# One decoder trunk on one core: product pairs added in one PSUM bank, tokens scaled before they are turned, kept projection weights, later folds, and a tail by 256 tokens

## The chip, the cores and the metric

The kernel runs on one core of a Trainium2 chip. The metric is the device time of one execution in microseconds (us): 2147.15 us before, the median of three runs (2144.82 to 2148.33). The engines are called as the profile calls them: PE (TensorE's matmuls), PEld (its weight loads), DVE (VectorE), ACT (ScalarE), POOL (GpSimd) and SP (SyncE, which issues most transfers).

## The reference, cut to what matters

The stream is 1024 tokens by 1024 channels in float32, and there are two layers. The first has a short gated convolution and a gated feed-forward network (FFN), the second multi-head latent attention and another FFN.

```python
h = h + short_conv_mixer(rms_norm(h, conv_norm_g), w_in, conv_w, w_out)   # u = h @ w_in, split in gate_b, gate_c, val
h = h + swiglu_ffn(rms_norm(h, conv_ffn_norm_g), w13, w2)                 # (silu(g) * u) @ w2
k_nope, k_pe, v = shared_mla_kv(h, ...)
h = h + mla_mixer(rms_norm(h, mla_norm_g), ...)                           # 8 heads, causal, then attn @ w_o
h = h + swiglu_ffn(rms_norm(h, mla_ffn_norm_g), w13, w2)
return rms_norm(h, final_norm_g)
```

`rms_norm` divides each token by the root of its mean square and multiplies by a gain per channel.

## The kernel before, in words

Channels lie on the 128 partitions and tokens run along the free dimension. Every float32 operand is cut in a high part, cast by ACT (L111, L306, L367), and a low part, the difference, made by DVE (L112, L307, L371). A product is then three matmuls in place of one (`three`, L152 to L155: high by high, high by low, low by high), each of 128x512.

The big weight products use a seven-product scheme on 2x2 blocks of weights and tokens. `Quad` is one pair of column blocks. Its seven products have the numbers 1, 2, 5, 6, 7, 4, 3, and each is 12 matmuls into a PSUM bank of its own (`product`, L422). After each, `evict` (L431) adds the bank to the result tiles C1 and C2: product 1 is copied by ACT (L437), 2 is added to it by DVE (L434), 5 is copied negated by ACT (L444) and subtracted by DVE (L445), 6 is subtracted by DVE (L447), and so on. `up` (L470) lays out the products of all quads, twelve for the convolution's input product and 22 for each FFN. The first seven quads (`head`) have their products 1 and 2 first, while the second half of the tokens is still being normed; the others run one after another. `Down` (L630) is the same scheme for the FFN's second product, with four banks per product and its operands loaded again from DRAM. `Plain` (L520) is the ordinary product for the output projections.

Between the stages stands a `Boundary` (L720). For each half of 512 tokens it squares the stream (ACT, L711), folds the squares of the channel blocks (DVE, L715), sums them over the partitions by matmuls with ones (`token_sums`, L214), makes one over the root (`rsqrt`, L194 to L206), spreads it by another matmul (`bcast`, L230), and multiplies it into the stream (DVE, L291).

The order is written out by hand. `Steps` holds a list of PE steps, and each other instruction is put before or after one of them; every engine then gets its instructions in that order and takes them strictly one after another. Only the attention is ordered by a scheduler. PSUM has eight banks of 128x512, handed out in turn. Raw weights have five buffers.

The places that are spoken of:

- **Beginning** (`first_x`, L830). Eight tiles of 128 tokens arrive. Four are turned by PE into channel order and written to DRAM as the residual (`raw_x`). The norm of the first 512 tokens is then multiplied in by a matmul with a diagonal matrix (L849). The second 512 are scaled as they lie (`scaled`, L866) before the second step, and turned (L880).
- **Attention's end**. The last three of the eight heads' outputs stay in SBUF. Their projection weights are loaded and cut by `Plain`, once for each half of the tokens and of the columns.
- **Tail** (from L1511). The second FFN's last product adds to the last 512 tokens by 512 channels. The final norm needs all of them, then come turns to token order (`out_turn`, L1518), the scaling (`out_store`, L1520) and the stores of 128x512 by SP (L1527).

Of the kernel before, what the change touches and what calls it, by code (L numbers as in the profile page):

```python
# [48 lines left out]
def trunk(ctx, tc, aps, out):  # L49
# [102 lines left out]
    def three(ps, wh, wl, xh, xl, st, en):  # L152
        nc.tensor.matmul(ps, lhsT=wh, rhs=xh, start=st, stop=False)  # L153
        nc.tensor.matmul(ps, lhsT=wh, rhs=xl, start=False, stop=False)  # L154
        nc.tensor.matmul(ps, lhsT=wl, rhs=xh, start=False, stop=en)  # L155
# [8 lines left out]
    vrows = half_tile("vrows")[:, :P]  # L164
    nc.vector.memset(vrows, 0.0)
    nc.scalar.dma_start(ident, A["ident"])
    col, r0 = {}, 0
    for nm in ("conv_norm_g", "conv_w", "conv_ffn_norm_g", "kv_norm_g", "mla_norm_g", "kv_latent_norm_g",
               "mla_q_norm_g", "mla_ffn_norm_g", "final_norm_g"):
        a = A[nm]  # L170
        if len(a.shape) == 3:
            a = a.rearrange("a b c -> (a b c)")
        elif len(a.shape) == 2:
            a = a.rearrange("a b -> (a b)")
        n = a.shape[0] // P
        nc.gpsimd.dma_start(vrows[r0:r0 + n, :], a.rearrange("(r p) -> r p", p=P))
        col[nm] = r0
        r0 += n
# [15 lines left out]
    def rsqrt(sums, nt, dim):  # L194

        var = small.tile([P, KD], F32, name="var")[:, :nt]
        nc.vector.tensor_scalar(var, sums, 1.0 / dim, EPS, ALU.mult, ALU.add)
        r = small.tile([P, KD], F32, name="r")[:, :nt]
# [147 lines left out]
    class Quad:  # L346


        def __init__(self, wv, ca, cb, first, done, eng):

            self.wv, self.ca, self.cb, self.first, self.done, self.eng = wv, ca, cb, first, done, eng
            self.W, self.bank, self.early, self.made = {}, {}, False, None

# [33 lines left out]
        def half(self, i):  # L387

            if i in (5, 7, 3):
                self.box = hi_tile("w_hi"), lo_tile("w_lo")  # L390
            (hi, lo), o = self.box, 512 if i in (6, 4) else 0
# [30 lines left out]
        def product(self, i, X):  # L422
            h, l, o = self.W[i]
            self.bank[i] = ps1("q")
            for c in range(4):
# [3 lines left out]
                three(self.bank[i], h[:, ws], l[:, ws], xh[:, cs], xl[:, cs], c == 0, c == 3)  # L429

        def evict(self, name):  # L431

            b = self.bank.pop(name)
            add = lambda o, a: nc.vector.tensor_tensor(o, b, a, ALU.add)  # L434
            if name == 1:
                self.C1 = work("c1")
                nc.scalar.copy(out=self.C1[:, 512:], in_=b)  # L437
            elif name == 2:
# [19 lines left out]
        def add(self, steps, op, name):  # L458
# [4 lines left out]
            if name == 3:  # L463
                for j, fn in enumerate(self.done):
                    steps.after(n + 1 + j, lambda fn=fn: fn(self.C1, self.C2))
# [4 lines left out]
    def up(steps, quads, op):  # L470
# [5 lines left out]
        for x, i in [(a, 1), (b, 1), (a, 2), (b, 2), *((x, i) for x in head[2:] for i in (1, 2)),  # L476
                     *((x, i) for i in (5, 6, 7, 4, 3) for x in (a, b)),
                     *((x, i) for x in quads[2:] for i in ((5, 6, 7, 4, 3) if x in head else (1, 2, 5, 6, 7, 4, 3)))]:
            n[x, i] = x.add(steps, op, i)
        for x in head:  # L480
            if not x.early:
                steps.before(n[x, 1] - 9, x.load_a)
                steps.before(n[x, 1] - 3, x.pair_hi)
                steps.before(n[x, 1] - 2, x.pair_lo)
        for x in quads:
# [8 lines left out]
            else:  # L494
                steps.before(n5 - 11, x.load_a)
                steps.before(n5 - 10, x.load_b)
                steps.before(n5 - 6, x.pair_hi)
                steps.before(n5 - 5, x.pair_lo)
# [21 lines left out]
    class Plain:  # L520


        def __init__(self, steps, wv, groups, x, final):
            self.ends = []
# [4 lines left out]
        def product(self, steps, wv, groups, x, final, t, cb):  # L529
            banks, tail = [], []  # L530
            for g, ks in enumerate(groups):
# [11 lines left out]
                def one(c, q, box=box, g=g, ks=ks):  # L543
                    if not banks:
                        banks.extend(ps1("pl") for _ in range(4))
                    wh, wl = box["w"]
                    xh, xl = x.get(t, g, c)
                    ws = slice(c * 512 + q * P, c * 512 + (q + 1) * P)
# [4 lines left out]
                steps.before(s - 7, load)  # L553
                steps.before(s - (1 if tail else 2), parts)
                if cb == 0:
                    x.prepare(steps, s, t, g)
                if cb and g >= len(groups) - 2:
# [46 lines left out]
    class Kept:  # L604


        def __init__(self, O, groups):
            self.O, self.groups = O, groups
# [4 lines left out]
        def get(self, t, g, c):  # L613
            return [x[:, t * 512:(t + 1) * 512] for x in self.O[self.groups[g][c] - self.groups[0][0]]]
# [15 lines left out]
    class Down:  # L630


        def __init__(self, steps, m, ws, nk, w, final, keep=True):
# [7 lines left out]
        def product(self, steps, i):  # L641
            wb, mb, outs = SEVEN[i]
            banks, tail = [], []
            for g, ks in enumerate(self.groups):
# [24 lines left out]
                def one(c, q, box=box, ks=ks):  # L669
# [4 lines left out]
                    cs, ws = slice(c * 512, (c + 1) * 512), slice(c * 512 + q * P, c * 512 + (q + 1) * P)  # L674
                    three(banks[q], wh[:, ws], wl[:, ws], mh[:, cs], ml[:, cs], k == 0, k == self.half - 1)
# [8 lines left out]
                if i == 6 and g >= len(self.groups) - 2:  # L684
                    tail += [lambda q, c=c, one=one: one(c, q) for c in range(len(ks))]
                    continue
                for c in range(len(ks)):
                    s = steps.add(lambda c=c, one=one: [one(c, q) for q in range(4)])
            for q in range(4 if tail else 0):
# [13 lines left out]
    class Norm:  # L703


        def __init__(self):
            self.sq = [[], []]

        def add(self, n, t):
            sq = work("nsq")[:, :512]  # L710
# [3 lines left out]
            if len(a) > 2:  # L714
                nc.vector.tensor_tensor(a[0], a[0], a.pop(1), ALU.add)  # L715
# [4 lines left out]
    class Boundary:  # L720


        def __init__(self, gname):
            self.op, self.norm = Operand(gname), Norm()
# [14 lines left out]
        def second(self, steps, n):  # L739

            steps.before(n + 1, lambda: setattr(self, "d", diag(half_tile, self.norm.sums(1), 4)))
            steps.before(n + 3, lambda: setattr(self, "R1", bcast(self.d, 1)[0]))
            todo = self.op.second(lambda f, kk: self.op.block(f, 1, kk, self.R1))
            for m, fn in zip((3, 4, 5, 6, 6, 7, 8, 9, 11, 12, 13, 14, 15, 16, 17, 18), todo):
# [63 lines left out]
    def gains():  # L808
        vps = ps1("vps")
        nc.tensor.transpose(vps[:, :r0], vrows[:r0, :], ident[:r0, :r0])  # L810
# [763 lines left out]
```

## Time and profile before

| | before |
|---|---|
| median of three runs | 2147.15 us |
| the profiled execution, its time | 2144.56 us |
| its span, first to last instruction | 2142.6 us |
| mean granted TensorE clock | 0.990 |
| granted clock, 0 to 50 us | 0.90 |
| granted clock, 1450 to 1500 us | 0.84 |
| granted clock, 2100 us to the end | 0.89 |

The views have one row per instruction or group: its start or count, its duration, its engine, its line of the kernel, the tile written and the tiles read. In square brackets, or behind a bar, stands the time for which the engine had been idle and what ended that. Matmuls overlap, so that the duration of one (some 0.39 us for 128x512) is longer than the distance between two. The place of the distance is taken from the starts.

### The profile page before, as it was taken

Reading aid. Unit: us, or ns where it says so; the run is one execution under the profiler, and the core shown is the slowest. Engines: PE = TensorE matmul, PEld = TensorE weight load, DVE = VectorE, ACT = ScalarE, POOL = GpSimd, SP = SyncE. Lnnn points to the kernel's source line nnn. Section 1 sums busy time; section 2 is a strip of 40 time slices with the busy share of each in tenths; the row PEclk is TensorE's granted clock in tenths of the full one; section 3 lists DMA queues with packets and bytes.
Section 4 is the critical chain, followed back from the end, with each engine's and each line's share of the span. In section 5 each row is a group of like instructions: output and inputs, shape, how many; then the busy total and the mean of one; then the engine's idle time right before and its main releaser. Section 6 shows DMA issues by size and latency. Waiting matters only on the chain. (4 is left out here: it accounts for less than half of the span.)

```text
span 2142.6 us, 25826 instructions
## 1 busy us (share of the span) xinstructions
PE 2079.4 (97%) x9553; PEld 1712.4 (80%) x9553; DVE 1526.0 (71%) x2275; ACT 845.0 (39%) x1418; POOL 305.0 (14%) x413
## 2 busy tenths in 40 slices
PE   7999999999999999999999999989999999999997
PEld 6878888878888887787888887867878888888786
DVE  5897656977777778867577787357887777767545
ACT  6423344523333333354245455224433333333444
POOL 2233210121112210000013332100111111100000
PEclk9999999999999999999999999998999999999999
DMA  6354775476866686564122224225478475685542
GB/s 210 84 118 118 214 282 175 108 194 192 193 161 152 147 277 230 192 235 144 58 68 68 65 72 154 98 93 162 148 177 189 146 162 168 149 323 191 176 167 98
DMA packets 275565, 340.55 MB, mean 159 GB/s; under 512 B 18143, under 2 KB 178080, under 8 KB 275120
## 3 DMA queue, kind: packets, MB, share of 16 engines
q1 hardware_dynamic: 241376, 264.28, 37.9%
q0 software_dynamic: 33920, 74.57, 16.4%
q8 instruction: 74, 1.21, 0.2%
q14 instruction: 51, 0.42, 0.1%
q10 hardware_dynamic: 144, 0.07, 0.0%
HBM read 261.79 MB, written 126.35 MB: 181 GB/s over the span
## 5 line engine op out<-in xcount | busy, mean ns | idle before, releaser
L155 PE MATMUL q<-xh,w_lo 128*128 128x512 f32 x1568 | 614.6, 392 | 5.0 <-DVE w_lo L112 2.8
L153 PE MATMUL q<-xh,w_hi 128*128 128x512 f32 x1568 | 615.3, 392 | 1.5 <-ACT w_hi L111 1.5
L154 PE MATMUL q<-xl,w_hi 128*128 128x512 f32 x1568 | 612.5, 391 | 2.1 <-DVE xl L307 2.1
L155 PEld LDWEIGHTS q<-xh,w_lo 128*128 128x128 f32 x1568 | 295.4, 188 | 75.2 <-DVE w_lo L112 11.8
L153 PEld LDWEIGHTS q<-xh,w_hi 128*128 128x128 f32 x1568 | 295.6, 188 | 65.4 <-ACT w_hi L111 4.8
L154 PEld LDWEIGHTS q<-xl,w_hi 128*128 128x128 f32 x1568 | 295.7, 189 | 64.3 <-DVE xl L307 2.9
L112 DVE TENSOR_TENSOR w_lo<-wr,w_hi 128x512 fp32r<-128x512 f32 (+1 forms) x272 | 194.5, 715 | 162.4 <-ACT w_hi L111 162.3
L111 ACT CAST w_hi<-wr 128x512 fp32r<-128x512 f32 (+1 forms) x272 | 169.7, 627 | 286.9 <-DVE wr L385 136.7
L155 PE MATMUL dn<-mp_hi,wp_lo 128*128 128x512 f32 x616 | 242.6, 394 | 4.9 <-DVE wp_lo L112 3.2
L153 PE MATMUL dn<-mp_hi,wp_hi 128*128 128x512 f32 x616 | 242.3, 393 | 0.5 <-ACT wp_hi L111 0.5
L154 PE MATMUL dn<-mp_lo,wp_hi 128*128 128x512 f32 x616 | 240.8, 391 | 0.7 <-DVE mp_lo L112 0.7
L973 POOL COPY paced<-pace 128x1 f32<-128x1 f32 x128 | 73.7, 576 | 959.4 <-ACT pace L972 959.4
L112 DVE TENSOR_TENSOR mp_lo<-m,mp_hi 128x1024 fp32r<-128x1024 f32 x84 | 95.3, 1134 | 129.5 <-ACT mp_hi L111 129.5
L111 ACT CAST mp_hi<-m 128x1024 fp32r<-128x1024 f32 x84 | 82.2, 979 | 214.9 <-PE dn L154 206.4
L155 PEld LDWEIGHTS dn<-mp_hi,wp_lo 128*128 128x128 f32 x616 | 115.9, 188 | 36.3 <-DVE wp_lo L112 12.3
L154 PEld LDWEIGHTS dn<-mp_lo,wp_hi 128*128 128x128 f32 x616 | 116.0, 188 | 25.6 <-DVE mp_lo L112 1.1
L153 PEld LDWEIGHTS dn<-mp_hi,wp_hi 128*128 128x128 f32 x616 | 116.1, 188 | 24.8 <-ACT wp_hi L111 1.8
L456 ACT ACTIVATE c<-c 128x512 f32<-128x512 f32 x44 | 27.8, 632 | 234.9 <-DVE c L434 234.9
L434 DVE TENSOR_TENSOR c<-q,c 128x512 f32<-128x512 f32 x112 | 77.0, 687 | 49.4 <-PE q L155 44.8
L112 DVE TENSOR_TENSOR wp_lo<-w,wp_hi 128x1024 fp32r<-128x1024 f32 x84 | 94.8, 1128 | 0.0
L111 ACT CAST wp_hi<-w 128x1024 fp32r<-128x1024 f32 x84 | 81.9, 975 | 0.0
L1368 ACT ACTIVATE p<-ps_s,mx,rq 128x128 f32<-128x128 f32 (+3 forms) x64 | 53.3, 834 | 59.3 <-DVE mx L1365 54.1
(289 smaller groups left out, 3337.6 us busy)
## 6 DMA issues: line engine op xcount, KB each, us to landing
m<-md_f SPq DMA_DIRECT2D x70, 512.0 KB, 4.9
md_f<-c SPq DMA_DIRECT2D x110, 256.0 KB, 3.6
wr<-in_conv_ffn_w_dram SPq DMA_DIRECT2D x47, 512.0 KB, 6.5
wr<-in_mla_ffn_w_dram SPq DMA_DIRECT2D x47, 512.0 KB, 5.3
w<-mw_f SPq DMA_DIRECT2D x40, 512.0 KB, 3.7
h<-hd SPq DMA_DIRECT2D x32, 512.0 KB, 8.4
wr<-in_conv_w_in_dram SPq DMA_DIRECT2D x31, 512.0 KB, 5.6
mw_f<-in_conv_ffn_w_dram POOLq DMA_DIRECT2D x30, 512.0 KB, 7.1
```

Of the source, the lines that this page charges most:

```text
L111: nc.scalar.copy(out=hi, in_=src)
L112: (eng or nc.vector).tensor_tensor(lo, src, hi.bitcast(F32), ALU.subtract)
L153: nc.tensor.matmul(ps, lhsT=wh, rhs=xh, start=st, stop=False)
L154: nc.tensor.matmul(ps, lhsT=wh, rhs=xl, start=False, stop=False)
L155: nc.tensor.matmul(ps, lhsT=wl, rhs=xh, start=False, stop=en)
L434: add = lambda o, a: nc.vector.tensor_tensor(o, b, a, ALU.add)
L456: nc.scalar.activation(self.C1[:, 512:], self.C1[:, 512:], self.first)
L973: nc.gpsimd.tensor_copy(b, a)
L1368: nc.scalar.activation(p[:, :kw], ps[:, :kw], AF.Exp, bias=mx, scale=rq[:, qb:qb + 1], accum_out=rsum)
```

## The change

1. `up` gives every quad `onto = {2: 1, 6: 5}`: product 2 goes on in product 1's bank and 6 in 5's. The bank of 1 is copied by ACT before 2 begins, and then holds 1 + 2, which ACT takes out alone; 5 is no longer subtracted, and 6's eviction takes 5 + 6. Two DVE operations per quad go. So that ACT has a product's time for its copy, the order becomes 1, 5, 2, 6, 7, 4, 3, and 5, 4, 6, 7, 3 for the rest of the head quads.
2. The first 512 tokens are scaled as they lie too, in two halves of the channels, and turned by the identity. The fourth tile's residual is put off, the convolution's gain comes in a transfer of its own, and the squares, the norm and the scaling of the second 512 tokens go two to four steps later. The first two quads' convolution steps are spread (`apart = 2`).
3. The projection weights of heads 5 to 7 are loaded whole during the last head, cut once, and kept in six tiles.
4. At that boundary the squares of the second half of the tokens are not folded as they come, but by four folds some steps later (`later=True`), and the weights of the first two FFN quads are loaded and cut eight steps earlier (`up(..., 8)`).
5. The last three channel blocks of the last `Down` product run by 256 tokens (`finish_half`), each half with its own norm and stores; the first half's stores before it are closer together.

```diff
-        dg = half_tile("dg")
-        diagonals(dg, xs[0], 4)
         conv_quads[0].pair_hi()
+        scaled(0, slice(0, 512))
         conv_quads[0].pair_lo()
-        squares(4, 5)
...
+        first_block(0, 0)
+        first_block(0, 1)
+        xop.advance()
+        raw_store(3, last, (nc.vector, nc.scalar))
+        conv_quads[1].pair_hi()
+        scaled(0, slice(512, S))
+        conv_quads[1].pair_lo()
...
-    steps.before(1, scaled)
...
+    steps.before(1, lambda: first_block(1, 0), lambda: first_block(1, 1), xop.advance)
+    steps.before(2, lambda: squares(4, 5), lambda: gains(1))
+    steps.before(3, lambda: squares(6, 7), lambda: norms(1))
+    steps.before(4, lambda: scaled(1, slice(0, S)))
...
         def product(self, i, X):
             h, l, o = self.W[i]
-            self.bank[i] = ps1("q")
+            j = self.onto.get(i)
+            self.bank[i] = ps1("q") if j is None else self.bank[j]
...
         def evict(self, name):
+            elif name == 2 and name in self.onto:
+                nc.scalar.activation(self.C1[:, :512], b, self.first)
...
-                nc.vector.tensor_tensor(self.C1[:, 512:], self.C1[:, 512:], b, ALU.subtract)
+                if 6 not in self.onto:
+                    nc.vector.tensor_tensor(self.C1[:, 512:], self.C1[:, 512:], b, ALU.subtract)
...
+        for x in quads:
+            x.onto = {2: 1, 6: 5}
+        lead = [(x, i) for j in range(0, FILL, 2) for i in (1, 2) for x in head[j:j + 2]]
...
-                     *((x, i) for x in quads[2:] for i in ((5, 6, 7, 4, 3) if x in head else (1, 2, 5, 6, 7, 4, 3)))]:
+                     *((x, i) for x in quads[2:] for i in ((5, 4, 6, 7, 3) if x in head else (1, 5, 2, 6, 7, 4, 3)))]:
...
+    for k in (5, 6, 7):
+        wo_load(k)
+    wo_parts(5)
     for u in pend:
         pv(*u)
...
-    bd = Boundary("mla_ffn_norm_g")
-    pl = Plain(steps, kp(flat(A["mla_w_o"])), pairs(5, H), Kept(O1, pairs(5, H)), bd.norm.add)
+    bd = Boundary("mla_ffn_norm_g", later=True)
+    for j, k in enumerate((6, 7)):
+        steps.before(j, lambda k=k: wo_parts(k))
+    pl = Plain(steps, None, [[5], [6], [7]], Kept(O1), bd.norm.add, wo_kept)
...
-    n0 = up(steps, quads2, bd.op)
+    n0 = up(steps, quads2, bd.op, 8)
...
+                for th in range(2):
+                    for q in range(4):
+                        s = steps.add(lambda q=q, th=th: [fn(q, halves[th]) for fn in tail])
+                        steps.after(s, lambda q=q, th=th: self.by_half(q, th, lambda: add(q, th)))
...
+    steps.after(n + 7, last_mean, lambda: out_turn(5, 1), lambda: out_store(5, 1), lambda: out_store(4, 1), last_rows,
+                *[lambda a=a: out_turn(*a) for a in ((6, 0), (7, 0), (6, 1), (7, 1))],
+                *[lambda a=a: out_store(*a) for a in ((6, 0), (7, 0), (6, 1), (7, 1))])
```

The order on ACT at the beginning, before: from the last cast of the first 512 tokens to the scaling of the second 512 (`sq` are squares of token tiles `xt`, `c1` a product's copy, `w_hi` a cut weight whose raw tile is `wr`).

```order
L306 CAST xh_267<-xraw_254 128x1024
L852 ACTIVATE xraw_270<-xps_271,vec_69 128x512
L852 ACTIVATE xraw_270<-xps_277,vec_69 128x512
L306 CAST xh_284<-xraw_270 128x1024
L803 ACTIVATE sq_288,xsum_98<-xt_124 128x1024
L803 ACTIVATE sq_290,xsum_98<-xt_126 128x1024
L199 ACTIVATE r_294<-var_292 128x4
L437 COPY c1_322<-q_309 128x512
L367 CAST w_hi_324<-wr_303 128x1024
L870 ACTIVATE xt_122<-xt_122,rs_301 128x1024
L870 ACTIVATE xt_126<-xt_126,rs_301 128x1024
```

And now, from the first product's copy on:

```order
L451 COPY c1_277<-q_264 128x512
L378 CAST w_hi_279<-wr_256 128x1024
L929 ACTIVATE xraw_281<-xps_288,vec_69 128x512
L316 CAST xh_294<-xraw_281 128x1024
L929 ACTIVATE xraw_297<-xps_304,vec_69 128x512
L316 CAST xh_311<-xraw_297 128x1024
L451 COPY c1_328<-q_315 128x512
L378 CAST w_hi_332<-wr_258 128x1024
L872 ACTIVATE sq_334,xsum_98<-xt_120 128x1024
L872 ACTIVATE sq_336,xsum_98<-xt_122 128x1024
L453 ACTIVATE c1_277<-q_264 128x512
L872 ACTIVATE sq_358,xsum_98<-xt_124 128x1024
```

The squares of the second 512 tokens now stand behind two casts of weights, and the third quad's cast `w_hi_279` ahead of the operands of product 2. The bank `q_264` is read twice, after product 1 and after product 2.

The order on DVE at the boundary behind the attention, before: from the adding of the second half's first channel blocks (`h` from the banks `pl`) to the second quad operand (`xl` is the low part of an FFN operand, `nsq` a fold of squares).

```order
L715 TENSOR_TENSOR nsq_12221<-nsq_12221,nsq_12241 128x512
L291 SCALAR_TENSOR_TENSOR xraw_12252<-h_11455,vec_69,R0_12202 128x512
L291 SCALAR_TENSOR_TENSOR xraw_12252<-h_11495,vec_69,R0_12202 128x512
L569 TENSOR_TENSOR h_11455<-h_11455,pl_12146 128x512
L715 TENSOR_TENSOR nsq_12221<-nsq_12221,nsq_12245 128x512
L569 TENSOR_TENSOR h_11741<-h_11741,pl_12228 128x512
L715 TENSOR_TENSOR nsq_12221<-nsq_12221,nsq_12269 128x512
L307 TENSOR_TENSOR xl_12250<-xraw_12224,xh_12249 128x1024
L291 SCALAR_TENSOR_TENSOR xraw_12282<-h_11701,vec_69,R0_12202 128x512
L291 SCALAR_TENSOR_TENSOR xraw_12282<-h_11741,vec_69,R0_12202 128x512
L371 TENSOR_TENSOR w_lo_12285<-wr_12106,w_hi_12255 128x1024
L569 TENSOR_TENSOR h_11495<-h_11495,pl_12147 128x512
```

And now, at the same place:

```order
L595 TENSOR_TENSOR h_11586<-h_11586,pl_12092 128x512
L301 SCALAR_TENSOR_TENSOR xraw_12115<-h_11340,vec_69,R0_12065 128x512
L301 SCALAR_TENSOR_TENSOR xraw_12115<-h_11380,vec_69,R0_12065 128x512
L595 TENSOR_TENSOR h_11340<-h_11340,pl_12017 128x512
L595 TENSOR_TENSOR h_11626<-h_11626,pl_12093 128x512
L595 TENSOR_TENSOR h_11380<-h_11380,pl_12018 128x512
L595 TENSOR_TENSOR h_11706<-h_11706,pl_12094 128x512
L317 TENSOR_TENSOR xl_12113<-xraw_12087,xh_12112 128x1024
L301 SCALAR_TENSOR_TENSOR xraw_12154<-h_11586,vec_69,R0_12065 128x512
L301 SCALAR_TENSOR_TENSOR xraw_12154<-h_11626,vec_69,R0_12065 128x512
L595 TENSOR_TENSOR h_11746<-h_11746,pl_12095 128x512
L317 TENSOR_TENSOR xl_12152<-xraw_12115,xh_12151 128x1024
```

The folds and the cut of the weights have left this stretch; what remains between the operands are the adds of `h` and the multiplications.

The order on PE at the program's end, before (`dn` are the last product's banks, `fps` turns to token order, `sp` sums for the norm):

```order
L154 MATMUL dn<-mp_lo,wp_hi 128x512
L155 MATMUL dn<-mp_hi,wp_lo 128x512
L1518 MATMUL fps<-ident,h 128x128 x9
L214 MATMUL sp<-ones,nsq 128x1 x8
L1518 MATMUL fps<-ident,h 128x128 x7
```

And now:

```order
L154 MATMUL dn<-mp_lo,wp_hi 128x256
L155 MATMUL dn<-mp_hi,wp_lo 128x256
L224 MATMUL sp<-ones,nsq 128x1 x2
L1644 MATMUL fps<-ident,h 128x128 x4
L224 MATMUL sp<-ones,nsq 128x1 x2
L1644 MATMUL fps<-ident,h 128x128 x16
```

Behind the last product stand four sums in two pieces, where eight stood, and all turns of the last 256 tokens.

More of the change, by code (lines that the diff above doesn't have):

```diff
@@ L464, in add, with up @@
                 for j, fn in enumerate(self.done):
-                    steps.after(n + 1 + j, lambda fn=fn: fn(self.C1, self.C2))
+                    steps.after(n + 1 + j * self.apart, lambda fn=fn: fn(self.C1, self.C2))
             return n
     FILL = 7
-    def up(steps, quads, op):
+    def up(steps, quads, op, ahead=0):
         head, n0 = quads[:FILL], len(steps.pe)
@@ L520, in trunk, with __init__ @@
     class Plain:
[L523 to L524 removed]
+        def __init__(self, steps, wv, groups, x, final, kept=None):
+            self.ends, self.kept = [], kept
             for t in range(2):
@@ L552, in product @@
                 s = len(steps.pe)
-                steps.before(s - 7, load)
-                steps.before(s - (1 if tail else 2), parts)
+                if kept is None:
+                    steps.before(s - 7, load)
+                    steps.before(s - (1 if tail else 2), parts)
                 if cb == 0:
                     x.prepare(steps, s, t, g)
-                if cb and g >= len(groups) - 2:
+                if cb and (g >= len(groups) - 2 or kept is not None):
                     tail += [lambda q, c=c, one=one: one(c, q) for c in range(len(ks))]
@@ L684, in product @@
                 if i == 6 and g >= len(self.groups) - 2:
-                    tail += [lambda q, c=c, one=one: one(c, q) for c in range(len(ks))]
+                    tail += [lambda q, *ts, c=c, one=one: one(c, q, *ts) for c in range(len(ks))]
                     continue
@@ L703, in trunk, with __init__, fold, flush @@
     class Norm:
-        def __init__(self):
-            self.sq = [[], []]
-        def add(self, n, t):
+        def __init__(self, later=False):
+            self.sq, self.two, self.later = [[], []], {}, later
+        def fold(self, t):
+            a = self.sq[t]
+            nc.vector.tensor_tensor(a[0], a[0], a.pop(1), ALU.add)
+        def flush(self, t):
+            while len(self.sq[t]) > 1:
+                self.fold(t)
+        def add(self, n, t):
+            if t and self.later:
+                if n % 2 == 0:
+                    self.two[n // 2] = work("nsq")
+                    self.sq[1].append(self.two[n // 2])
+                nc.scalar.activation(self.two[n // 2][:, n % 2 * 512:n % 2 * 512 + 512], st.h[n][:, 512:], AF.Square)
+                return
             sq = work("nsq")[:, :512]
@@ L739, in second @@
         def second(self, steps, n):
-            steps.before(n + 1, lambda: setattr(self, "d", diag(half_tile, self.norm.sums(1), 4)))
-            steps.before(n + 3, lambda: setattr(self, "R1", bcast(self.d, 1)[0]))
+            m = 1
+            if self.norm.later:
+                for j in range(3):
+                    steps.before(n + 1 + j, lambda: self.norm.fold(1))
+                steps.before(n + 4, self.norm.last)
+                m = 5
+            steps.before(n + m, lambda: setattr(self, "d", diag(half_tile, self.norm.sums(1), 4)))
+            steps.before(n + m + 2, lambda: setattr(self, "R1", bcast(self.d, 1)[0]))
             todo = self.op.second(lambda f, kk: self.op.block(f, 1, kk, self.R1))
-            for m, fn in zip((3, 4, 5, 6, 6, 7, 8, 9, 11, 12, 13, 14, 15, 16, 17, 18), todo):
+            at = (8, 9, 9, 10, 11, 11, 12, *range(13, 22)) if self.norm.later else (3, 4, 5, 6, 6, 7, 8, 9, *range(11, 19))
+            for m, fn in zip(at, todo):
                 steps.before(n + m, fn)
```

238 lines of the change are left out of this document (148 added, 90 removed).

## The prediction

> **What bounds the kernel now.** I read the page first, then the busy time by stretches, then who PE waited for, and then the order of time at four places.
>
> ```profile
> span 2142.6 us, 25826 instructions
> PE 2079.4 (97%) x9553; PEld 1712.4 (80%) x9553; DVE 1526.0 (71%) x2275; ACT 845.0 (39%) x1418; POOL 305.0 (14%) x413
> ```
>
> PE is busy for nearly the whole span, so what can be won is what PE loses, and where.
>
> ```profile
> 0.00:50.00 50.00, 35.51 (x195) 31.11 (x196) 27.61 (x43) 33.23 (x49) 9.13 (x18) 0.90 0.71 224
> 100.00:150.00 50.00, 46.88 (x195) 35.42 (x193) 45.17 (x52) 14.29 (x27) 22.45 (x19) 1.00 0.54 120
> 450.00:500.00 50.00, 49.43 (x213) 39.08 (x212) 39.93 (x62) 16.48 (x35) 11.09 (x16) 1.00 0.81 196
> 1550.00:1600.00 50.00, 49.42 (x213) 39.21 (x212) 41.07 (x64) 13.72 (x28) 7.70 (x10) 1.00 0.80 199
> ...
> 1464.00:1490.00 26.00, 20.77 (x71) 15.77 (x70) 17.54 (x28) 10.20 (x15) 0.87 (x2) 0.74 0.60 189
> 1490.00:1550.00 60.00, 60.00 (x267) 49.66 (x266) 53.71 (x63) 29.38 (x46) 10.12 (x14) 1.00 0.42 129
> 2086.00:2104.00 18.00, 13.84 (x60) 11.14 (x59) 10.50 (x14) 10.36 (x14) 0.00 (x0) 0.91 0.53 185
> ```
>
> The columns after the stretch are PE, PEld, DVE, ACT and POOL with their counts, then the granted clock. From 1490 to 1550 nothing is lost: 267 matmuls of 128x512 in 60 us, one in 0.225 us, 222 in 50 us. By that rate 100 to 150 lost 27 matmuls or 6.1 us with DVE busy for 90%, 450 to 500 and 1550 to 1600 lost 2.0 us each. Most of the span runs at the full rate and can't be made faster by taking work off DVE or ACT.
>
> ```profile
> PE xps L880 <- DVE xt L872: 5.4, 1, 5.4
> PE fps L1518 <- DVE o L1526: 4.2, 1, 4.2
> ...
> PE ps_wo L146 <- DVE h L1444: 2.1, 1, 2.1
> ...
> PE q L155 <- DVE w_lo L371: 2.0, 1, 2.0
> ```
>
> The waits (total, times, longest) are few and sit at the beginning, at the boundary behind the attention and in the tail, and there the clock falls too.
>
> **The bank shared by two products.** It takes two DVE operations off each of 56 quads.
>
> ```profile
> L434 DVE TENSOR_TENSOR c<-q,c 128x512 f32<-128x512 f32 x112 | 77.0, 687 | 49.4 <-PE q L155 44.8 <-ACT xraw L881 3.1 <-issue 0.5
> L437 ACT COPY c<-q 128x512 f32<-128x512 f32 x56 | 32.8, 586 | 59.3 <-PE q L155 59.3
> ```
>
> Half of the first row goes, and as many subtractions of like shape: 112 x 0.69 = 77 us of DVE, nearly all of it hidden behind PE. It pays where DVE is late. In 100 to 150 some 2.65 quads run (50 us over 84 matmuls x 0.225), so DVE sheds 3.6 us of 45, and the first two quads' convolution steps no longer fall together: of 6.1 us lost I take 4 back (1 to 6). In the two FFN heads (450, 1550) I take back 3 of 4, between 2 lost and 4 won, as the new order 5, 4, 6, 7, 3 asks for its weights in another rhythm. The cover is one product: product 2 waits for ACT's copy of 1, which takes 0.59 us, while PE has 12 x 0.225 = 2.7 us of another product. The second row says that ACT stood waiting for PE ahead of these copies.
>
> **The beginning.**
>
> ```profile
> 10.40 0.19 ACT L803 ACTIVATION_READ_ACCUMULATOR sq<-xt 128x1 f32 x1
> 24.75 1.26 ACT L852 ACTIVATE xraw<-xps,vec 128x512 f32<-128x512 f32 x2
> 28.05 1.04 ACT L803 ACTIVATE sq<-xt 128x1024 f32<-128x1024 f32 x1
> 29.42 0.20 ACT L199 ACTIVATE r<-var 128x4 f32<-128x4 f32 x1 [0.24 <-DVE var L197]
> 30.00 1.05 ACT L367 CAST w_hi<-wr 128x1024 fp32r<-128x1024 f32 x1
> 30.94 2.19 ACT L870 ACTIVATE xt<-xt,rs 128x1024 f32<-128x1024 f32 x2
> ...
> 47.86 1.03 PE L880 MATMUL xps<-ident,xt 128*128 128x128 f32 x8
> ```
>
> ```profile
> L356 SPq DMA_DIRECT2D wr<-in_conv_w_in_dram x2: 486/4074/7663, 10.4 to 10.9; - x2
> ...
> DMA to landing us min/median/max: 15.9/16.5/17.1
> ```
>
> Before, the last turn ends at 48.9, with five products done. Now ACT carries the chain to the second half's norm. Behind the squares (10.6) it has two casts of weights and two of operands (0.95 apart, by 30.00 to 30.94), four scalings of 512 and two evictions (0.6 each, by the two in 1.26) and two copies (0.59): 8.6 us, and with some 3 us of waits for DVE's norm, PE's turns and the first product this ends at 22. Then stands the third quad's cast. Its transfer was issued at 10.4 and landed 15.9 later, at 26.3. The fourth tile's residual, written to DRAM ahead of it before, now comes later; I take 25. From there come two evictions, four casts, two copies and the four squares (1.05 each): 1.2 + 3.8 + 1.2 + 4.2 = 10.4, with some 1 us of waits 36.4. The norm takes 1.5 (29.42 to 30.94), two scalings 2.2: 40.1. The next turns, 1.03, end at 41.1, with the same five products done. Three groups of turns remain, 3.1 us, which before lay behind. So 48.9 - 44.2 = 4.7, and with a slow clock after waits I take 4 (1 to 8; 8 if the weights land by 22). The 32 diagonal matmuls, which the trace counts as 64, become 32 turns; that is inside this sum.
>
> **The attention's end and the boundary.** Two cuts of weights of 128x1024 now stand in DVE's queue around the last maximum, one of them ahead of the add of `h` on whose bank PE waited 2.1 us.
>
> ```profile
> L307 DVE TENSOR_TENSOR xl<-xraw,xh 128x1024 fp32r<-128x1024 f32 x42 | 52.1, 1243 | 2.8 <-ACT xh L306 2.8
> L715 DVE TENSOR_TENSOR nsq<-nsq 128x512 f32<-128x512 f32 x36 | 24.6, 684 | 0.1
> L569 DVE TENSOR_TENSOR h<-h,pl 128x512 f32<-128x512 f32 x32 | 21.7, 682 | 25.9 <-PE pl L155 25.9
> L291 DVE SCALAR_TENSOR_TENSOR xraw<-h,vec,R 128x512 f32<-128x512 f32 x16 | 11.2, 743 | 0.0
> ...
> 1396.70 0.73 PE L1361 MATMUL ps_s<-kh,qnh 128*128 128x512 f32 x2 [2.61 <-ACT p L1368]
> 1399.21 1.05 PE L1361 MATMUL ps_s<-KL,qrs 128*128 128x512 f32 x2
> ```
>
> By the first row, of a like shape, PE waits 1.2 us more there; the cuts that no longer stand ahead of the projection give some of it back, and a slow clock takes it: 1.5 lost in all (0 to 4). For a wait of 2.61 us was followed by matmuls 0.42 us apart (two in 1.05), some 1 us more in a handful. [...]
>
> From 1464 to 1490 stood 53 products, two spreads and 16 sums, which cost 55 x 0.225 + 2.0 (the sums in the tail, below) = 14.4; lost are 11.6, and about 1 in the first half's sums. Now the last DVE work before the first operand is an add and a low part, 0.6 + 1.2 after the twelfth step of the projection, while PE has nine matmuls or 2.0: no wait. The second operand comes behind two multiplications, one add and one low part, 1.3 + 0.6 + 1.2 = 3.1 us into a product that needs it after seven matmuls, 1.6: 1.5 lost. The other two follow after 1.3 + 1.2 + a fold of 1.2 + 1.2 at 8.0 us, where PE asks at 4.2 + 2.7 + 1.6 = 8.5. With two more folds, their last half and two weights (5.5 us) DVE is through at 13.5, and PE's sums stand at 4.2 + 4 x 2.7 = 15; half the sums go, 0.9. So 12.6 - 1.5 - 1 (clock) + 0.9 = 11 won, 9.5 with the attention's end (6 to 13).
>
> **The tail.**
>
> ```profile
> 1099.69 0.28 PE L1322 MATMUL ps_v<-wv_lo,lat_part 128*128 128x256 f32 x1
> 1099.81 0.28 PE L1323 MATMUL ps_v<-wv_hi,lat_part 128*128 128x256 f32 x1
> ...
> 2097.90 1.12 PE L1518 MATMUL fps<-ident,h 128*128 128x128 f32 x4 [4.16 <-DVE o L1526]
> ...
> 2129.31 0.69 DVE L696 TENSOR_TENSOR h<-h,dn 128x512 f32<-128x512 f32 x1 [0.75 <-PE dn L155]
> 2130.03 0.63 ACT L711 ACTIVATE nsq<-h 128x512 f32<-128x512 f32 x1 [0.66 <-DVE h L696]
> 2130.65 1.95 PE L214 MATMUL sp<-ones,nsq 128*128 128x1 f32 x16 [0.24 <-DVE nsq L715]
> 2132.64 0.16 DVE L197 TENSOR_SCALAR var<-sp 128x4 f32<-128x4 f32 x1 [2.04 <-PE sp L214]
> 2134.08 2.73 DVE L1526 TENSOR_SCALAR o<-fps,rs 128x512 f32<-128x512 f32 x4
> 2134.79 4.46 SPq L1527 DMA_DIRECT2D out_dram<-o  x8
> ```
>
> The wait of 4.16 us came as the last early store stood in DVE's queue behind the next product's operands, and its bank was wanted. The stretch from 2086 to 2104 has 48 products and 12 turns (0.11 each, as eight take 1.03 with the end of the last): 12.1 of 18 us, so 5.9 lost. The stores now end two steps before that product, and all of it goes; if not, 4 come back. From the last matmul (2129.3) to the norm's root chain were 3.3 us, then 1.4, then eight evictions on two engines and eight stores of 0.56 in line, with the end at 2142.6, 13.3 later. Now an add and a square of 256, 0.4 each by half of the rows above and their fixed share, and a quarter of the sums, 0.5: chain at 1.8, rows at 3.2, first store at 4.0, the fourth 1.7 later at 5.7. Before, 3.4 us passed from the last store's issue (2139.2) to the end; that makes 9.1. So 4.2 are won. Of 36 matmuls come 72 of 0.12 in place of 0.113: 0.5 lost; sums and turns inside the product 0.5 more; the first half's eight sums fewer win 0.9. In all 10 (6 to 12).
>
> **The sum.** 4 + 4 + 3 + 9.5 + 10 = 30.5 us off the profiled execution's 2144.56, which gives 2114.1. That execution lies 2.6 below the median of the runs, 2147.15; against the median the forecast is 2116.6. A difference of 0.2%, 4.3 us, is about what a measurement here can tell from none.
>
> **The rivals.**
> - *The banks tie PE to ACT* (slower, 5%). Every quad now has two places at which PE may not go on before ACT has copied, 112 in all. If ACT is late by 0.5 us at each, behind a cast that waits for DVE, that costs 56 us and gives 2172. It decides from 30.5 / 112 = 0.27 us on. For it: ACT takes its work strictly in order, and DVE makes it wait for long. Against it: the copy stands ahead of the next cast, and had 59.3 us of its own waiting for PE.
> - *The wait at the beginning only moves* (17%). The squares stand behind weights that may land at 26.3 or later, and ACT's chain with them; nothing is won there: 2120.6.
> - *DVE was not the limit* (15%). What 100 to 150 and the heads lose stays (7 us), and at the boundary the late operands cost half of what is won (5): 2128.6.
> - *Shorter waits leave the clock alone* (10%). The 1 us at the boundary, 1 at the attention's end and 1 at the beginning, charged for waits of under 3 us, are not paid: 2113.6. [...]
>
> The forecast has 53%. The range 2105 to 2130 takes in the second to fourth rival and most of the bounds of the five terms, whose lows together make 12 and whose highs 43, seldom all at once. Only the first rival is on the other side: slower 0.05, within 0.2% 0.02, faster 0.93.
>
> **What would show it.** By its profile: at the beginning, the sixth product would start near 41 with three groups of turns to come; a start at 37 or 45 shows ACT's chain wrong. From 100 to 150, 210 matmuls or more. At the boundary, one short wait for `xl` and a clock above 0.9; at the attention's end `ps_wo` would wait 3 us and more. In the tail no wait for `fps`, and 9 us from the last `dn` to the end. The forecast is wrong if PE waits for ACT's copies of products 1 or 5, or if the waits that go are replaced by others in the same stretch.

## The result, and the profile after

The changed kernel takes 2123.55 us, median of four runs (2121.33 to 2126.17), where the kernel before took 2147.7 in the same runs. The ratio is 0.9891, with a 95% interval of 0.9877 to 0.9906. The forecast was 2116.6 (2105 to 2130): the direction and the range hold, but a quarter of the gain, 7 us, did not come. Runs that were disturbed are left out of all times: in the first experiment one of four took 3111 us, at a granted clock of 0.62. The profiled execution of the kernel after took 2122.53 us. From its page:

```profile
PE 2066.0 (97%) x9542; PEld 1706.4 (80%) x9542; DVE 1460.6 (69%) x2175; ACT 858.0 (40%) x1439; POOL 315.2 (15%) x412
```

Before, the span was 2142.6: 22.0 us are gone, where the terms added up to 30.5. To see where, I compare the start of the same PE step in both traces. Products are counted in the order in which PE runs them.

| step that starts | before | after | won so far | won in this stretch | forecast |
|---|---|---|---|---|---|
| 17th product of the convolution | 78.67 | 71.13 | 7.5 | 7.5 (beginning) | 4 |
| 66th product | 218.67 | 213.57 | 5.1 | -2.4 (convolution) | 4 |
| 148th product | 541.35 | 533.50 | 7.9 | 2.8 (first FFN head) | 1.5 |
| latent products | 1006.26 | 998.58 | 7.7 | -0.2 | 0 |
| last `ps_wo` matmul | 1416.55 | 1411.83 | 4.7 | -3.0 (attention's end) | -1.5 |
| 246th product | 1497.62 | 1480.42 | 17.2 | 12.5 (boundary) | 11 |
| 311th product | 1677.21 | 1657.67 | 19.5 | 2.3 (second FFN head) | 1.5 |
| last `dn` matmul | 2128.88 | 2110.91 | 18.0 | -1.6 (up to it) | 5.8 |
| end of the span | 2142.6 | 2120.6 | 22.0 | 4.0 (behind it) | 4.2 |

Two stretches failed, the convolution's first quads and the last product up to its last matmul. The same stages as windows of the kernel after (stretch, then PE, PEld, DVE, ACT and POOL with their counts, then the granted clock):

```profile
100.00:150.00 50.00, 46.36 (x194) 36.82 (x193) 43.56 (x51) 16.16 (x31) 20.82 (x19) 0.97 0.51 111
442.00:492.00 50.00, 50.00 (x221) 41.23 (x220) 41.30 (x62) 16.85 (x35) 11.43 (x16) 1.00 0.88 223
1458.10:1484.10 26.00, 24.67 (x111) 19.81 (x110) 20.20 (x28) 15.70 (x22) 5.69 (x4) 1.00 0.78 239
2043.00:2060.00 17.00, 15.05 (x70) 12.20 (x69) 8.60 (x16) 10.09 (x13) 0.00 (x0) 0.90 0.31 107
```

From 1458 to 1484, which answers to 1464 to 1490 before, 111 PE instructions fit where 71 did, at full clock. Both heads run at the full rate, the first with 221 matmuls in 50 us as shown, the second with 222 from 1534 to 1584. But 100 to 150 still has 194 matmuls where 210 were forecast, and a new slow place stands at 2043. Whom PE waited for after the change (total, times, longest):

```profile
PE ps_wo L146 <- DVE h L1521: 3.5, 1, 3.5
...
PE sp L224 <- DVE nsq L754: 2.8, 2, 2.0
...
PE q L153 <- ACT w_hi L111: 2.6, 3, 1.8
...
PE q L153 <- ACT c L460: 1.9, 2, 1.1
```

The wait for `fps` (4.2) is gone, and so are those of 2.0 for `w_lo` and 2.1 for `xl` at the boundary. In their place stand a longer wait for `h` at the attention's end, one for the sums (`sp`), and two for the copy `c` of product 5: the shared bank ties PE to ACT there. The longest of the three for a cast of weights (`w_hi`), 1.8 us, is new too; it stands in the convolution, where no wait was longer than 1.3 us before.

### The profile page after: what moved, and what is told of

Read it like the earlier page. It is cut to its first block, busy times and chain, and to the rows that moved or that the text cites. A ratio compares the mean times of both kernels' runs of the same rounds, so it can differ in the third digit from the quotient of the medians.

```text
span 2120.6 us, 25572 instructions
## 1 busy us (share of the span) xinstructions
PE 2066.0 (97%) x9542; PEld 1706.4 (80%) x9542; DVE 1460.6 (69%) x2175; ACT 858.0 (40%) x1439; POOL 315.2 (15%) x412
## 4 chain that ended last, share of the span: by engine, by line
PE 83%; DVE 7%; DMA 4%; ACT 3%; issue 2%; SPq 0%; POOL 0%; DVEq 0%; ACTq 0%; POOLq 0%
PE q L154 16%; PE q L153 16%; PE q L155 16%; PE dn L155 4%; PE dn L154 4%; PE dn L153 4%; PE ps_s L1438 4%; PE pl L155 2%; PE pl L153 2%; PE pl L154 2%; DVE wp_lo L112 1%; PE ps_t L1460 1%; PE ps_l L155 1%; PE ps_l L153 1%; PE ps_l L154 1%
## 5 line engine op out<-in xcount | busy, mean ns | idle before, releaser
L155 PE MATMUL dn<-mp_hi,wp_lo 128*128 128x512 f32 (+1 forms) x628 | 245.3, 391 | 6.3 <-DVE wp_lo L112 4.5
L153 PE MATMUL dn<-mp_hi,wp_hi 128*128 128x512 f32 (+1 forms) x628 | 244.3, 389 | 1.0 <-ACT wp_hi L111 1.0
L154 PE MATMUL dn<-mp_lo,wp_hi 128*128 128x512 f32 (+1 forms) x628 | 243.3, 387 | 0.9 <-DVE mp_lo L112 0.9
L1050 POOL COPY paced<-pace 128x1 f32<-128x1 f32 x128 | 84.8, 663 | 923.0 <-ACT pace L1049 923.0
L382 DVE TENSOR_TENSOR w_lo<-wr,w_hi 128x1024 fp32r<-128x1024 f32 x56 | 68.7, 1226 | 7.6 <-ACT w_hi L378 7.6
L738 DVE TENSOR_TENSOR h<-h,dn 128x512 f32<-128x512 f32 x108 | 68.7, 679 | 0.0
```

The costliest lines, as they stand in the source:

```text
L153: nc.tensor.matmul(ps, lhsT=wh, rhs=xh, start=st, stop=False, **more)
L155: nc.tensor.matmul(ps, lhsT=wl, rhs=xh, start=False, stop=en, **more)
L382: nc.vector.tensor_tensor(lo, self.ra, hi.bitcast(F32), ALU.subtract)
L738: nc.vector.tensor_tensor(hv, hv, banks[q], ALU.add if sign > 0 else ALU.subtract)
L1050: nc.gpsimd.tensor_copy(b, a)
```

## The experiments

All are edits of the kernel after. "After" in what follows is its profile above, of 2120.6 us span.

**The tail's sums.** In the kernel after, DVE's queue around 2046:

```profile
2046.11 1.23 DVE L112 TENSOR_TENSOR mp_lo<-m,mp_hi 128x1024 fp32r<-128x1024 f32 x1 [1.87 <-ACT mp_hi L111]
2047.25 1.22 DVE L112 TENSOR_TENSOR wp_lo<-w,wp_hi 128x1024 fp32r<-128x1024 f32 x1
2048.39 0.69 DVE L754 TENSOR_TENSOR nsq<-nsq 128x512 f32<-128x512 f32 x1
```

and PE behind it:

```profile
2049.13 1.05 PE L224 MATMUL sp<-ones,nsq 128*128 128x1 f32 x8 [1.95 <-DVE nsq L754]
...
2050.50 0.63 PE L154 MATMUL dn<-mp_lo,wp_hi 128*128 128x512 f32 x1
2050.93 0.63 PE L155 MATMUL dn<-mp_hi,wp_lo 128*128 128x512 f32 x1
```

The change halves the 16 sums by one more fold (`flush`), and that fold waits in the queue behind two low parts. The matmuls after it start 0.43 us apart instead of 0.227.

```diff
-    steps.before(e[4] + 3, lambda: fnorm.flush(0))
+    steps.before(e[4] + 2, lambda: fnorm.flush(0))
```

> The last fold of the first half's squares in the tail is placed one step earlier, ahead of the two low parts of the next operands; nothing else is changed from the changed kernel (2123.6 us, span 2120.6). Theory: this fold, which stood behind those two low parts, is what made the sums wait 1.95 us at 2049 and the clock fall behind them (8 matmuls 0.43 apart, 1.6 us): the wait goes, the clock there stays full, span 2117.0, ratio to before 0.9875. Rival: the two low parts are late as well, and PE waits for them as long as it did for the sums: span within 1 of 2120.6.

> The kernel with the earlier fold alone once more, since its first profile was disturbed. Theory: no wait of the sums, full clock behind them, span 3.6 below the changed kernel's in the same call. Rival: PE waits for the low parts of the next operands instead: within 1 of it.

Measured (k1): 2118.63 us (median of three), ratio 0.9872 (0.9854 to 0.989), and once more (k11) 2119.21, 0.9871 (0.9855 to 0.9888), beside 2124.17 for the kernel after. These rows are of k11, DVE and then PE:

```profile
2044.94 0.69 DVE L754 TENSOR_TENSOR nsq<-nsq 128x512 f32<-128x512 f32 x1 [0.18 <-ACT nsq L768]
```

```profile
2047.29 0.40 PE L155 MATMUL dn<-mp_hi,wp_lo 128*128 128x512 f32 x1
2047.53 0.95 PE L224 MATMUL sp<-ones,nsq 128*128 128x1 f32 x8
```

The fold ends before the sums are due, PE goes from the last product straight into them, and the matmuls behind keep the full rate (granted clock 1.00 from 2043 to 2062). From the last `q` to the last `dn` it takes 226.86 us (1881.07 to 2107.93), after 230.43 (1880.48 to 2110.91): 3.6 won, as the theory had it.

**The tail's early stores.**

```diff
-            steps.before(e[4] + 6 + (2 * tb + q + 1) // 2, lambda tb=tb, q=q: (out_turn(tb, q), out_store(tb, q)))
+            steps.before(e[4] + 6 + 2 * tb + q, lambda tb=tb, q=q: (out_turn(tb, q), out_store(tb, q)))
```

> The early stores of the first half go back to one in each step, as before; the rest is the changed kernel's. Theory: the wait for fps that the denser stores took away had covered operands that VectorE and ScalarE deliver late; with the wait back (4.2 us and a slow clock, 5.9 together) the waits from 2080 to 2101 (2.75 us) are gone: span 2123.8. Rival: the two have nothing to do with each other: the waits from 2080 to 2101 stay, the 5.9 come on top, span 2126.5.

Measured (k6): 2126.1 us, ratio 0.9905 (0.9889 to 0.992), with a span of 2122.6. The wait is back:

```profile
2080.55 1.11 PE L1644 MATMUL fps<-ident,h 128*128 128x128 f32 x4 [4.16 <-DVE o L1652]
```

and these two of the kernel after, the larger part of what PE lost from 2080 to 2101, are gone:

```profile
2086.92 0.50 PE L153 MATMUL dn<-mp_hi,wp_hi 128*128 128x512 f32 x1 [0.49 <-ACT wp_hi L111]
2088.37 0.50 PE L155 MATMUL dn<-mp_hi,wp_lo 128*128 128x512 f32 x1 [0.64 <-DVE wp_lo L112]
```

From the last `q` to the last `dn` it takes 233.10 us (1879.86 to 2112.96), 2.7 more than after: the theory's 3.2, not the rival's 5.9. The removed wait had covered operands that DVE and ACT deliver late, and about half of its price comes back.

**The beginning.**

```diff
         for x in conv_quads[:2]:
             x.load_a()
+        conv_quads[2].load_a()
         for tb in range(4, KD):
             load_x(tb)
...
```

> At the beginning the third quad's first weights are asked for ahead of the second four token tiles instead of behind them. Theory: the chain to the sixth product hangs on their landing at 23.55 us, for which ScalarE stood 2.09 us: they land by 18, the sixth product starts near 36.5 in place of 38.35, span 2118.7. Rival: what PE does not wait for there it waits for behind (turns, squares of tiles that now land 2 us later): sixth product at 38 or later, span within 0.7 of 2120.6.

Measured (k7): 2124.19 us, ratio 0.9896 (0.9878 to 0.9914). In the kernel after, on ACT:

```profile
23.58 1.05 ACT L378 CAST w_hi<-wr 128x1024 fp32r<-128x1024 f32 x1 [2.09 <-DMA wr<-in_conv_w_in_dram]
```

The sixth product starts at 38.35. With the weights asked for earlier, ACT and then PE:

```profile
21.22 1.05 ACT L378 CAST w_hi<-wr 128x1024 fp32r<-128x1024 f32 x1
```

```profile
36.00 0.49 PE L153 MATMUL q<-xh,w_hi 128*128 128x512 f32 x1
100.73 0.50 PE L153 MATMUL q<-xh,w_hi 128*128 128x512 f32 x1 [1.70 <-ACT c L460]
```

It comes 2.35 us earlier, so the chain did hang on that landing. At the 66th product 1.1 are left (212.46 against 213.57): the last row is the wait for the copy `c`, 0.79 in the kernel after, that took part of it. By the whole time nothing is won that can be measured: the span is 2120.8, as the rival had it, though its sixth product is the theory's.

**The convolution's first quads.** Here DVE, POOL, ACT and PE of the kernel after have to be read side by side:

```profile
96.87 2.31 DVE L826 TENSOR_TENSOR c<-c,c 128x1024 f32<-128x1024 f32 x1
99.10 0.68 DVE L448 TENSOR_TENSOR c<-q,c 128x512 f32<-128x512 f32 x1
99.71 1.18 DVE L393 TENSOR_TENSOR wr<-wr 128x512 f32<-128x512 f32 x1
```

```profile
96.49 1.61 POOL L387 TENSOR_TENSOR wr<-wr 128x512 f32<-128x512 f32 x1
98.18 2.16 POOL L390 TENSOR_TENSOR wr<-wr 128x512 f32<-128x512 f32 x1
```

```profile
100.92 0.62 ACT L111 CAST w_hi<-wr 128x512 fp32r<-128x512 f32 x1 [5.28 <-DVE wr L393]
101.45 0.59 ACT L460 ACTIVATE c<-q 128x512 f32<-128x512 f32 x1
```

```profile
102.09 0.50 PE L153 MATMUL q<-xh,w_hi 128*128 128x512 f32 x1 [0.79 <-ACT c L460]
```

DVE's multiplication takes 2.31 us; the same one at 102.18 takes 1.22. It ends 1.08 behind the end of POOL's first sum (98.10), a little less than those 1.22. Behind it DVE's sum of weights is late, behind that ACT's cast, and behind the cast the copy that frees the bank. Three edits take this chain apart. In k4, DVE makes POOL's sums:

```diff
+    for x in conv_quads[2:5]:
+        x.eng = nc.vector
```

> The weight sums of the third to fifth quad, six operations of 128x512, are made on VectorE instead of GpSimd. Theory: GpSimd's sums lengthen the VectorE work beside them (from 85 to 126 us low parts of 128x512 took 1.56 and 1.77 us in place of 0.69, products of 128x1024 2.31 in place of 1.21), about 5.3 us in five places, while six sums on VectorE cost 4.1: PE's waits from 85 to 126 us fall by 1 to 2, span 2119. Rival: VectorE is late by the mere amount of its work there, and six operations more make it later: waits longer by 2 to 4 us, span 2122.6 to 2124.6.

In k3, every product has its own bank:

```diff
-            x.onto = {2: 1, 6: 5}
+            x.onto = {}
```

> No product shares a bank, in any quad; the new order of the products and all else stay. Theory (VectorE's work was the limit where PE lost time in the quads): 112 more VectorE operations of 0.69 us bring back the waits of both heads (5.2 us) and lengthen those from 85 to 126 us by 2 to 4: span 2127.8 to 2130. Rival (the shared banks tie PE to ScalarE's copies from 100 to 117 us, and the heads won by the new order): the two waits for the copy c go, 1.9 us, the heads lose nothing: span 2118.7.

In k5, the convolution's steps stand further apart, and the gate's products five steps later:

```diff
-        x.apart = 2
+        x.apart = 3
+    conv_quads[2].delay = 5
...
```

> The convolution steps of the first two quads stand three steps apart instead of two, and the gate's products five steps later, with all else as in the changed kernel. Theory: VectorE's queue is crowded from 87 to 122 us by these twelve operations of 1.2 to 2.3 us, and the sums and low parts of weights behind them come late: spread wider, PE's waits there (7.2 us in six places) halve, span 2117. Rival: the copies on ScalarE that stand behind casts set the end, or the waits move to where the steps now stand: span within 1 of 2120.6.

The stretch from the 17th to the 66th product took 140.0 us before and 142.4 after. In four more profiles with the same code in that stretch it took 140.9 to 141.3. The difference lies behind the longest wait there, the one of 1.8 us, which is the same in all five. In the kernel after, DVE has four convolution steps (117.15 to 122.7) in front of a sum of weights (`wr`), on which ACT's cast waits, and PE on the cast. These are ACT's row, PE's, and the window behind it:

```profile
124.03 0.62 ACT L111 CAST w_hi<-wr 128x512 fp32r<-128x512 f32 x1 [6.52 <-DVE wr L396]
124.70 0.51 PE L153 MATMUL q<-xh,w_hi 128*128 128x512 f32 x1 [1.79 <-ACT w_hi L111]
120.00:135.00 15.00, 13.21 (x51) 10.01 (x50) 12.48 (x16) 4.71 (x9) 5.21 (x6) 0.89 0.77 196
```

and in k10, the same kernel once more:

```profile
124.19 0.50 PE L153 MATMUL q<-xh,w_hi 128*128 128x512 f32 x1 [1.80 <-ACT w_hi L111]
120.00:135.00 15.00, 13.20 (x57) 10.29 (x57) 13.50 (x17) 4.73 (x9) 6.72 (x6) 1.00 0.85 206
```

In the first the clock fell and eight matmuls ran 0.43 us apart, in the second it did not: 1.5 us for the same wait. So the price of the change there is 0.9 to 1.3 us, and 2.4 where the clock falls. It fell in k4 and k3 too (0.89 from 120 to 135 in both), so these are compared with the 142.4.

*k4:* 2119.02 us, ratio 0.987 (0.9855 to 0.9885), the stretch 139.9 (70.85 to 210.75). With POOL's sums gone, DVE's first multiplication reads:

```profile
96.05 1.22 DVE L826 TENSOR_TENSOR c<-c,c 128x1024 f32<-128x1024 f32 x1
```

The other one, at 99.76, takes 1.22 too, there is no wait for `c`, and 2.5 us are won, though DVE has six operations more. The theory holds. The wait of 1.8 us stays.

*k3:* 2126.02 us, ratio 0.99 (0.9886 to 0.9915), the stretch 146.1. In the quads that run product 5 ahead of 2, 5 is now subtracted before 2 is added to the copy of 1, so the output is not the reference's; all other counts and shapes are those of separate banks. The waits for `c` go, but others come (in the whole run; after, 2.6 for the first and 0.9 for the second):

```profile
PE q L153 <- ACT w_hi L111: 4.2, 5, 1.8
PE q L155 <- DVE w_lo L112: 3.5, 7, 0.8
```

So the shared bank is worth 3.7 us in that stretch, in spite of its tie. From the 246th to the 311th product k3 takes 180.0 us, after 177.3, before 179.6: the second head was won by the shared banks. From the 66th to the 148th it takes 320.3, after 319.9, before 322.7: there the banks are not needed for it. The theory held in two of three stretches; the span came out at 2123.8, 4 below it.

*k5:* 2122.98 us, ratio 0.9884 (0.9868 to 0.9901), the stretch 142.6, no less, though the clock did not fall: the waits at 116 and 122 went, the one for `c` at 102 grew to 1.7, and three of 0.5 to 1.6 us came at 134 to 145. So the steps do make the wait at 122, but spreading them further only moves the loss, as the rival had it. One step apart, as in the kernel before, was not tried.

**The attention's end.** In the kernel after (DVE, then PE):

```profile
1391.88 1.22 DVE L112 TENSOR_TENSOR wo_l<-wo_r,wo_h 128x1024 fp32r<-128x1024 f32 x1
1393.01 1.22 DVE L1441 TENSOR_REDUCE mx<-ps_s 128x1 f32<-128x1024 f32 x1
1394.14 1.21 DVE L1521 TENSOR_TENSOR h<-ps_wo,h 128x1024 f32<-128x1024 f32 x1
```

```profile
1395.41 1.22 PE L146 MATMUL ps_wo<-oth,wo_hi 128*128 128x512 f32 x2 [3.45 <-DVE h L1521]
...
1400.70 1.05 PE L146 MATMUL ps_wo<-oth,wo_hi 128*128 128x512 f32 x2
```

```diff
-        split(*wo_kept[k], wo_raw[k])
+        split(*wo_kept[k], wo_raw[k], eng=nc.gpsimd)
```

> The low parts of the three kept w_o weights are cut on GpSimd, which stands idle at the attention's end, so that VectorE's queue has none of them. Theory: it is these cuts, 1.2 us each, ahead of the add of h, that made the wait of ps_wo 3.45 us where it was 2.1 before, and the longer wait makes the clock fall (59 matmuls 0.273 apart, 2.7 us lost): wait 2.2, matmuls 0.227 apart, span 2116.7. Rival: GpSimd's cuts lengthen the VectorE work beside them, so the add ends no earlier: wait over 3 us, span 2120 to 2121.

Measured (k2): 2123.04 us, ratio 0.9892 (0.9876 to 0.9908).

```profile
1398.27 1.22 PE L146 MATMUL ps_wo<-oth,wo_hi 128*128 128x512 f32 x2 [2.14 <-DVE h L1521]
1399.29 1.05 PE L148 MATMUL ps_wo<-oth,wo_hi 128*128 128x512 f32 x2
```

In the kernel before the same wait was followed by the full rate, two matmuls in 0.62 us in place of 1.05:

```profile
1403.04 0.73 PE L146 MATMUL ps_wo<-oth,wo_hi 128*128 128x512 f32 x2 [2.14 <-DVE h L1444]
1403.61 0.62 PE L148 MATMUL ps_wo<-oth,wo_hi 128*128 128x512 f32 x2
```

The wait is back at its 2.1, so the cut in DVE's queue had made it longer. The time did not follow, and the span, 2123.2, is above theory and rival, as 3.7 us went in the first FFN head (told below). From the first latent product to the last `ps_wo` it took 412.7 us, after 413.3, since PE ran slowly behind the shorter wait too (granted clock 0.87 from 1380 to 1420). The theory's second half, that the longer wait is what slows the clock, fell.

**Together, and the kernel after once more.** k8 has the edits of k1, k2, k4 and k7; k9 those of k1, k4 (with the sums of the third to eighth quad) and k7.

> Four edits together on the changed kernel: the last fold of the tail's first half a step earlier, the kept w_o weights' low parts on GpSimd, the sums of the third to fifth quad on VectorE, and the third quad's weights asked for ahead of the second four token tiles. Theory (each takes away a wait of its own place): 3.6 at the fold, 2.3 at the beginning, 2.5 from 85 to 126 us with no wait for the copy c that took back 1.2 when the weights came early, 1.2 of the wait at the attention's end: 9.6 in all, span 2111.0, ratio 0.9846. Rival (the gains feed later waits: the early weights bring the crowded quads nearer, the clock takes the attention's end): half of it, span 2115.5.

> As the one before, but the w_o cuts stay on VectorE, and the sums of the third to eighth quad, not of the third to fifth, are made on VectorE. Theory: from the sixth quad on PE waited for nothing, so the other three quads' sums change nothing, and the attention's end costs what it did: span 2112.2. Rival: twelve more sums of 0.69 us make VectorE late from 126 to 200 us: span 2114 or more.

> The changed kernel once more, for how far two profiles of one kernel differ at the places told here: by both theories the waits stand as they did, ps_wo 3.45, sums 1.95, copies c 0.8 and 1.1; the slow clock behind them may differ by 1 to 2 us: span 2118.5 to 2122.5, ratio 0.989.

Measured side by side: k8 2115.56 us, 0.9855 (0.9842 to 0.9868); k9 2113.7, 0.9844 (0.983 to 0.9859); the kernel after 2124.17, 0.9898 (0.9884 to 0.9913). Both beat it, by 8.6 and 10.5 us. k8's span, 2113.2, lies midway between theory and rival. k9's, 2115.3, is on the rival's side, but not by the rival's mechanism: the stretch from the 17th to the 66th product took 138.0 us there and 139.6 in k8, so the sums of the sixth to eighth quad cost something on POOL as well (in k8 a low part of 128x512 beside one of them took 1.76 us and PE waited 1.2 for it; in k9 it took 0.68 and PE did not wait), and the first FFN head took 321.8, for the reason that follows. k9's median is 3.5 below its profiled execution, 2117.15.

The second profile of the kernel after shows what the first had not (ACT, then PE):

```profile
445.98 0.60 ACT L460 ACTIVATE c<-q 128x512 f32<-128x512 f32 x1 [3.53 <-DMA md_f<-c]
```

```profile
446.62 0.50 PE L153 MATMUL q<-xh,w_hi 128*128 128x512 f32 x1 [1.95 <-ACT c L460]
```

The copy of product 5 needs a buffer that is still being written out, and product 6 waits for the copy. It was so in 5 of the 10 profiles with that code: there the first FFN head, 66th to 148th product, took 321.8 to 323.7 us, in the other five 319.9 to 320.3. Before it took 322.7. The last experiment gives product 6 its own bank in two quads of each FFN head:

```diff
-            x.onto = {2: 1, 6: 5}
+            x.onto = {2: 1} if x in quads[2:4] and x.eng is nc.vector and x not in conv_quads else {2: 1, 6: 5}
```

> Three edits on the changed kernel (the tail's last fold a step earlier, sums of the third to fifth quad on VectorE, the third quad's weights ahead of the second four token tiles), and in the third and fourth quad of both FFN heads product 6 has a bank of its own again. Theory: the wait for the copy c near 444 us, 0 to 2.1 us from one profile to the next, comes of the shared bank: the copy of product 5 stands until a buffer is written out, and product 6 behind it; with its own bank product 6 does not wait: no wait of more than 0.5 us from 400 to 500 us, whatever the transfer does, span 2111.5 to 2113.5, ratio 0.984. Rival: the bank of product 5 is missing a product or two later, so the same wait stands there: 1 to 3 us lost from 400 to 500 us where the transfer is late, span 2113.5 to 2115.5.

Measured (k12): 2116.76 us, 0.9859 (0.9842 to 0.9875), the head 319.8 us without a wait. But the copy had stood for its buffer only 0.99 us in this profile, and after a stand of 1.44 PE lost nothing either. It is consistent with the theory and tells nothing apart. The span, 2115.4, is in the rival's range without the rival's wait: from the 148th product to the latent products it took 466.8 us, after 465.1.

## Why the prediction was right, and where it was wrong

- **Beginning** (forecast 4 in 1 to 8, got 7.5). The mechanism was right and the size too small: the third quad's weights were taken to hold ACT until 25, and the cast began at 23.58; the sixth product came at 38.35, not 41, with the three groups of turns still to come. k7 shows that this landing sets it. The rival that the wait only moves did not come.
- **Convolution** (forecast 4 won, got 1 to 2.4 lost). The step that failed is "DVE sheds 3.6 us of 45 ... of 6.1 us lost I take 4 back". What was shed was worth 3.7 us (k3), near the forecast, with the two waits for a late copy (1.9) already paid; but the step left out what the rest of the change does there. With banks of its own k3 took 146.1 us against 140.0 before, so the rest costs some 6 us. Of these 1.5 are the clock behind the wait of 1.8 us, and that wait, which the kernel before does not have, comes of the convolution's steps in front of a sum of weights (it went in k5). DVE's busy time from 100 to 150 went from 45.17 to 43.56 only, and part of that goes with POOL's sums: the first multiplication takes 2.31 us beside them and 1.22 in k4, without them. What else makes DVE late there stays open: the new order of the products, the earlier start and the distance of two steps in place of one weren't tried apart.
- **Heads** (forecast 3, got 5.1). Both run without loss in this profile, the second by the banks; the first without them too (k3), and what won it wasn't tried apart. In the first the gain hangs on a transfer, and in half of the profiles it is gone.
- **Attention's end and boundary** (forecast 9.5, got 9.5). The wait for `ps_wo` is 3.45 and the one short wait for `xl` 1.33, as written; the end lost 3.0 and not 1.5, and the boundary won 12.5 and not 11. That the two misses cancel is luck. The added 1.2 us of waiting was worth 0.6 us when k2 took it away again; most of the loss is the clock, which fell there with either wait.
- **Tail** (forecast 10, got 2.5). The end behind the last matmul was right (4.0 against 4.2). The failed steps are "the first half's eight sums fewer win 0.9", where the fold for it cost 3.6 (k1), and "all of it goes", where the wait for `fps` went but half of its price came back from operands that it had covered (k6).
- **The rivals.** "The banks tie PE to ACT" was given 112 places at 0.5 us; it happened at two places, behind a cast that waits for DVE, as described, and at a third in half of the profiles, behind a buffer, for 2 to 4 us in all. "Shorter waits leave the clock alone" was half right. At the boundary, its first place, the clock stayed full behind a wait of 1.33 us (1.00 from 1458 to 1484). But waits of 1.95 and 1.79 us (before 2049 and 124) were followed by matmuls 0.43 apart, while behind the 2.61 us at the attention's end, which had slowed the clock in the kernel before (two matmuls in 1.05 us), it stayed full in the kernel after (two in 0.63).

## What to carry to other kernels

When a wait is removed, look at what had become ready during it: the next late operand gives part of the price back (about half in k6). An operation that saves work on the busy engine can cost more than it saves when it stands one place too late in another engine's queue, as the fold in the tail did (3.6 us in k1, for a saving put at 0.9). And a bank shared by two products was here only as quick as the slowest step that frees it: a cast (waits of 0.79 and 1.07 us in the profile after), and at times a write to DRAM (1.95 in k10). Last, two profiles of a stretch compare only where the clock did the same behind the same wait in both: the 1.8 us at 122 came with a granted clock of 0.89 in one and 1.00 in the other, 1.5 us apart.

## What the runs showed of the hardware

- DVE's multiplication of 128x1024 with both operands in SBUF took 2.31 us beside GpSimd's sums (96.87 above) and 1.22 without them (k4, 96.05); an add that reads PSUM (99.10 above) kept its 0.68 beside the second sum. What in the sums lengthens the one and not the other was not shown.
- The clock behind one and the same wait differs between runs. Behind 1.8 us at 122 it fell in 4 of the 11 profiles that have this wait (0.97 from 100 to 150 in these four, 1.00 in the others). Behind 3.45 us at the attention's end seven pairs of matmuls ran slowly in the profile after, and three in k6:

```profile
1397.95 1.22 PE L146 MATMUL ps_wo<-oth,wo_hi 128*128 128x512 f32 x2 [3.45 <-DVE h L1521]
...
1400.67 0.69 PE L146 MATMUL ps_wo<-oth,wo_hi 128*128 128x512 f32 x2
```

  What sets the moment of the change was not shown. The seven pairs took 6.14 us (1395.41 to 1401.55), and seven at the full rate behind them 3.19 (1402.06 to 1405.25). So the wait of 3.45 us in the profile after cost its length and 3.0 us on top, the one of 1.80 us in k10 its length and nothing that shows behind it (granted clock 1.00).
